# A down-projection whose plain features are split over two rounds of products, with feature reads paced per product and an unscaled residual

## The chip, the cores and the metric

One core of one Trainium2 chip runs the whole kernel. The metric is the device time of one execution in microseconds (us), as the median of several runs. The engines are named as the profile names them: PE is TensorE (matrix products), DVE is VectorE, ACT is ScalarE, POOL is GpSimd and SP is SyncE, which only issues transfers here.

## What is computed

One decoder layer over 1032 tokens (1024 of a prompt, 8 of a sample), 1024 features wide, in float32:

```
h <- LN1(alpha*h + 0.5*SwiGLU_1(h))
h <- LN2(alpha*h + W_o[ sig(g_a)*(A(h) W_ao) + sig(g_r)*(R(h) W_ro) ])
h <- LN3(alpha*h + 0.5*SwiGLU_2(h))

def swiglu(x, w_up, w_down):
    gate, up = jnp.split(x @ w_up, 2, axis=-1)
    return (jax.nn.silu(gate) * up) @ w_down
```

A is sliding-window attention and R is a retention; alpha is 2^(1/4), about 1.189. The hidden width of a SwiGLU is 2816, which is 22 tiles of 128. The change is about the two products with `w_down` (one in each feed-forward part) and about the factor alpha of the residual.

## The kernel before

**Products.** A float32 product is made of three TensorE products of halves: each operand is split into a rounded part `hi` and a rest `lo`, and hi·hi, hi·lo and lo·hi are added. The split of an operand tile is two instructions: ACT copies the tile into `hi` (line 112), then DVE subtracts `hi` from the tile (line 116). A weight half tile (128x512) is loaded by SP into one of 4 buffers `raw`; ACT writes `w_hi` and DVE `w_lo`, into one of 8 slots. A slot is free again when the last product that used its previous weight has run, so the ACT row that writes a `w_hi` waits for PE.

**Quads.** Most of the work runs in a scheme in which seven products stand for eight (Strassen-Winograd). Seven products, numbered 0 to 6, share a quad of four weight halves; three of their seven weight operands are sums of halves, which DVE makes in four instructions (tiles `st`). Their seven token operands lie split in seven buffers TT[0] to TT[6], the tiles T0 to T6. A product is 24 matmuls of 258 columns into one of three PSUM banks `pr`.

**The feed-forward part.** The up-projection ends with hidden tile 21. Its results leave the core's memory: six hidden tiles (groups 0 and 5) go to DRAM as they are (`adr`, plain features), the sixteen tiles of groups 1 to 4 as seven combinations per pair of groups (`tdr`, two rounds of seven features). The down-projection reads them back. It has four parts, in this order of the list `units` (lines 392 to 409):

- 16 plain units `dn` with group 0 (12 matmuls each): 8 for the output tiles d = 4 to 7 (the accumulator `yb`), then 8 for d = 0 to 3 (`ya`);
- round Q0: 4 quads, j = 0 to 3, of seven products `S` (groups 1 and 2);
- round Q1: 4 quads of seven products (groups 3 and 4);
- units `down` with group 5, one per output tile and chunk of tokens.

Each `dn` and `S` unit ends with an evacuation: DVE adds 0.25 times the bank to a half tile of `ya` or `yb`. In a quad the second product's bank is apart; products 0, 2, 4 and 6 follow one another in one bank, each adding to what stands there, and each of them waits until DVE has evacuated the one before.

**The residual.** `ya` and `yb` start as alpha times the residual. `yb` is in place early; `ya` is read back in `start_d` (2064 KB) when the first plain unit is due, and POOL multiplies it by alpha in 12 instructions (`alpha`, line 843).

**Reads and splits of features.** A feature read (`fetch_one`, lines 929 to 942) goes to a buffer that is no longer used. The table `qslot` says which buffer the feature of product i takes; it is the same in both rounds, so a buffer comes free for Q1 when its last product of Q0 has run. `fetch_after` lets a read start after a unit if 3.5 us of the kernel's own time estimate (FETCH) have passed since the last one. Each read starts a generator `split`: an ACT copy and a DVE subtraction for the first half of the tile, then for the second. `features` is called ahead of the product that needs the feature and puts out what is left of its split.

**The order of the work.** The instruction order on each engine is written out by the program itself: a class `E` keeps an estimate of each engine's time, generators are resumed when their time has come (`E.run`), and what an engine's queue holds then is fixed. Engines run their queues strictly in that order.

Of the kernel before, what the change touches and what calls it, by code (L numbers as in the profile page):

```python
# [18 lines left out]
P = 128  # L19
# [16 lines left out]
QUADS = [(1, 2), (3, 4)]  # L36
ORDER = [0, 1] + [GROUPS[g][k] for q in QUADS for k in range(4) for g in q] + GROUPS[5]
# [11 lines left out]
FETCH = 3.5  # L49
# [174 lines left out]
def build(tc, I, O):  # L224
# [3 lines left out]
    with ctx:  # L228
# [136 lines left out]
        def ffn_units(p, r0):  # L365
# [26 lines left out]
            n = 0  # L392
            for i in (1, 0):
                j = add_job(down[0] + i)
                for dd in range(4):
                    for hf in range(2):
                        units.append(dict(kind="dn", p=p, c=0, d=4 * i + dd, dd=dd, hf=hf, jobs=[j], first=n == 0, bank=(0, 2, 1)[n % 3]))
                        n += 1
            for q, (g1, g2) in enumerate(QUADS):
                for j in range(4):  # L400
                    a, b = down[g1] + j, down[g2] + j
                    for i, (x, h) in enumerate(add_quad([(a, 0), (b, 0), (a, 1), (b, 1)])):
                        quad_op[p, "S", q, j, i] = len(ops)
                        ops.append(dict(src=x, quad=h))
                        units.append(dict(kind="S", p=p, c=0, q=q, j=j, i=i, jobs=[]))
# [430 lines left out]
        def end_t(p):  # L836
# [6 lines left out]
            E.spawn(alpha_b())  # L843

        def alpha(t):
            for k in range(4):
                for c in range(3):
                    n0, N = CH[c]
                    E.pscale(t[:, k, n0:n0 + N], t[:, k, n0:n0 + N], ALPHA, n=N)

        def alpha_b():
            yield E.pe + 40.0
            alpha(env["yb"])
# [35 lines left out]
        def start_d(p):  # L889
# [8 lines left out]
            alpha(env["ya"])  # L898

        def end_quads(p):  # L900

            env["st"] = None
            open_banks([pairs.index(pr[i]) for i in (2, 0, 1)])
# [5 lines left out]
        qslot = [[4, 5, 6, 1, 2, 3, 0], [2, 3, 1, 4, 5, 6, 0]]  # L909
        fetches, fstate, rested, splits = [], dict(t=0.0), {}, {}  # L910

        def fill(p):

            res = [(0, ("U", 0), 0, k) for k in range(2)]
            res += [(s, ("U", s), "Q0", qslot[p].index(s)) for s in range(1, 7)]
            res.append((0, "dn", "Q0", 6))
            res += [(qslot[p][i], (0, i), "Q1", i) for i in range(7)]
            return res + [(qslot[p][i], (1, i), 5, 2 * i + k) for i in range(2) for k in range(2)]

        def split(i, hi, lo, n, t):  # L920
# [3 lines left out]
            for k in (0, g):  # L924
                t = E.act(hi[:, k:k + g], f(lo)[:, k:k + g], n=g)
# [3 lines left out]
        def fetch_one():  # L929
            p, i, _, g, k = fetches.pop(0)  # L930
            x = TT[i]
            if g in (0, 5):
                o = k % 2 * 2 * T
                hi, lo = x[:, o:o + T], x[:, o + T:o + 2 * T]
                ds(out=f(lo), in_=adr[p][k + (2 if g else 0)])
# [6 lines left out]
            splits.setdefault((i, g), []).append(E.spawn(split(i, hi, lo, n, E.dma(n * 0.000512))))  # L942

        def fetch_after(u):
# [10 lines left out]
            elif u["kind"] == "S" and u["j"] == 3:  # L955
                rested[u["q"], u["i"]] = True
            elif u["kind"] == "dn" and (u["d"], u["hf"]) == (3, 1):
                rested["dn"] = True
            while fetches and fetches[0][2] in rested and (E.pe > fstate["t"] + FETCH or fetches[0][4] % 2 and fetches[0][3] in (0, 5)):
                fetch_one()  # L960

# [498 lines left out]
        def evac_s(j, i, bank):  # L1460
# [3 lines left out]
            E.stt(yd, bank[:, :, 0:HC], 0.25, yd, ALU.mult, ALU.add, n=HT)  # L1464


        def evac(u, bank):
# [9 lines left out]
            elif kind == "dn":  # L1477
                k = u["hf"] * HT
                yd = v(Y(u["d"], k, k + HT))
                E.stt(yd, bank[:, :, 0:HC], 0.25, yd, ALU.mult, ALU.add, n=HT)  # L1480
            elif kind == "down":
                d = u["d"]
                yd = Y(d, n0, n0 + N)
                t = E.stt(yd, ps, 0.25, yd, ALU.mult, ALU.add, n=N)
# [129 lines left out]
        def before(ui, u):  # L1614
# [69 lines left out]
            if kind == "dn":  # L1684
                if u["first"]:
                    start_d(u["p"])
                features(u["p"], 0, 0)
# [265 lines left out]
```

## Time and profile before

| what | value |
|---|---|
| time, median of 3 runs | 2236.43 us (2235.77 to 2236.72) |
| the profiled execution's own time | 2237.71 us |
| its span, first to last instruction | 2235.9 us |
| PE busy | 2143.2 us, 96% of the span |
| DVE busy | 1483.8 us, 66% |
| ACT busy | 827.0 us, 37% |
| POOL busy | 233.7 us, 10% |
| first down-projection, start of the first plain unit | 467.08 us |
| second down-projection, start of the first plain unit | 1953.96 us |

How to read it: PE is busy nearly all the time, so a change can shorten the kernel only where PE stands still or runs slowly. In the rows of the timeline the first number is the start, the second the length, xN says how many instructions of one shape follow each other, and in brackets stands how long the engine stood idle ahead of them and for whom. "PEclk" is the granted clock of TensorE as a share of the full one.

### The profile page before, as it was taken

How to read it: one execution, taken by the hardware profiler on the slowest of the kernel's cores; microseconds unless marked ns; L12 is line 12 of the kernel's file. 1: busy time of each engine (PE TensorE's matmuls, PEld its weight loads, DVE VectorE, ACT ScalarE, POOL GpSimd, SP SyncE). 2: the span in 40 equal slices, each digit the busy share in tenths (PEclk: the TensorE clock that was granted, in tenths of full speed). 3: DMA queues.
4: the chain of work that ended last, by engine and by line, in shares of the span. 5: the costliest groups of instructions: out<-in, count | busy, mean ns of one | idle time of the engine just before them, and what ended most of it. 6: DMA issues, size and time to landing. Idle time of an engine off the chain costs nothing.

```text
span 2235.9 us, 39516 instructions
## 1 busy us (share of the span) xinstructions
PE 2143.2 (96%) x15865; PEld 2102.5 (94%) x15865; DVE 1483.8 (66%) x2675; ACT 827.0 (37%) x1561; POOL 233.7 (10%) x283
## 2 busy tenths in 40 slices
PE   8999999989899999999999999997999999989896
PEld 8999999989899889999979999997999999989896
DVE  7766666576656886556676747787666666676657
ACT  5333333342322575111324434554333333432323
POOL 1100000010004433111110202011000000010003
PEclk9999999999999999999999999999999999999998
DMA  4322323261421211111253434531332232353322
GB/s 141 107 96 86 113 92 109 73 244 60 171 101 37 66 41 35 44 40 40 77 189 130 139 123 133 185 113 54 103 105 91 96 110 91 133 180 109 118 97 76
DMA packets 111129, 231.81 MB, mean 104 GB/s; under 512 B 13666, under 2 KB 17602, under 8 KB 107090
## 3 DMA queue, kind: packets, MB, share of 16 engines
q1 hardware_dynamic: 110594, 229.24, 30.3%
q8 instruction: 125, 2.05, 0.4%
q14 instruction: 58, 0.48, 0.1%
q0 software_dynamic: 352, 0.05, 0.1%
HBM read 184.44 MB, written 45.84 MB: 103 GB/s over the span
## 4 chain that ended last, share of the span: by engine, by line
PE 55%; DVE 9%; DMA 3%; ACT 2%; issue 2%; POOL 1%; SPq 0%; DVEq 0%; POOLq 0%; ACTq 0%
PE pr L94 28%; PE mb L94 25%; DVE T L116 2%; DVE w_lo L116 1%; PE sb L94 1%; DVE ya L116 1%; DMA raw<-in_w_dram 1%; DVE yb L116 1%; DMA T<-tdr 1%; DVE ln L116 1%; DVE zt L116 1%; PE sb L102 1%; ACT w_hi L112 1%; ACT T L112 0%; DVE st L116 0%
## 5 line engine op out<-in xcount | busy, mean ns | idle before, releaser
L94 PE MATMUL pr<-T,w_hi 128*128 128x258 f32 x7008 | 1151.0, 286 | 54.0 <-DVE T L116 14.1
L94 PEld LDWEIGHTS pr<-T,w_hi 128*128 128x128 f32 x7008 | 979.7, 192 | 65.7 <-DVE T L116 17.2
L94 PE MATMUL pr<-T,w_lo 128*128 128x258 f32 x3504 | 714.8, 286 | 1.3 <-DVE w_lo L116 1.3
L94 PEld LDWEIGHTS pr<-T,w_lo 128*128 128x128 f32 x3504 | 553.0, 192 | 1.8 <-DVE w_lo L116 1.8
L94 PE MATMUL mb<-T,w_hi 128*128 128x384 f32 (+1 forms) x2208 | 528.2, 326 | 1.8 <-DVE yb L116 1.8
L116 DVE TENSOR_TENSOR w_lo<-raw,w_hi 128x512 fp32r<-128x512 f32 x500 | 357.3, 733 | 142.5 <-ACT w_hi L112 141.4
L112 ACT ACTIVATE w_hi<-raw 128x512 fp32r<-128x512 f32 x500 | 304.7, 625 | 270.2 <-PE pr L94 138.4
L94 PEld LDWEIGHTS mb<-T,w_hi 128*128 128x128 f32 x2208 | 380.1, 190 | 8.3 <-issue 4.7
L94 PE MATMUL mb<-T,w_lo 128*128 128x384 f32 (+1 forms) x1104 | 354.7, 321 | 0.0
L94 PEld LDWEIGHTS mb<-T,w_lo 128*128 128x128 f32 x1104 | 208.7, 189 | 0.0
L112 ACT ACTIVATE w_hi<-st 128x512 fp32r<-128x512 f32 x174 | 108.2, 629 | 181.5 <-DVE st L116 88.5
L116 DVE TENSOR_TENSOR a<-pr,a 128x516 f32<-128x516 f32 x87 | 60.5, 696 | 97.6 <-PE pr L94 93.9
L116 DVE TENSOR_TENSOR w_lo<-st,w_hi 128x512 fp32r<-128x512 f32 x174 | 116.0, 688 | 9.0 <-ACT w_hi L112 9.0
L136 POOL TENSOR_SCALAR ya<-ya 128x384 f32<-128x384 f32 (+1 forms) x24 | 16.2, 676 | 834.3 <-DMA ya<-hres 433.4
L112 ACT ACTIVATE a<-pr 128x516 f32<-128x516 f32 x86 | 51.5, 600 | 135.6 <-PE pr L94 135.6
L116 DVE SCALAR_TENSOR_TENSOR ya<-pr,ya 128x516 f32<-128x516 f32 x72 | 49.6, 691 | 76.5 <-PE pr L94 65.8
L112 ACT ACTIVATE T<-T 128x1032 fp32r<-128x1032 f32 (+1 forms) x80 | 72.2, 927 | 64.3 <-DMA T<-tdr 60.4
L116 DVE TENSOR_TENSOR T<-T 128x1032 fp32r<-128x1032 f32 (+1 forms) x80 | 85.1, 1080 | 15.3 <-ACT T L112 15.1
L116 DVE SCALAR_TENSOR_TENSOR yb<-pr,yb 128x516 f32<-128x516 f32 x72 | 49.4, 693 | 54.2 <-PE pr L94 54.2
L112 ACT ACTIVATE th<-a 128x516 f32<-128x516 f32 x43 | 27.3, 636 | 125.6 <-DVE a L116 125.6
L116 DVE SCALAR_TENSOR_TENSOR gt<-gt,mb 128x384 f32<-128x384 f32 (+1 forms) x48 | 24.3, 509 | 59.4 <-PE mb L94 57.8
L116 DVE TENSOR_TENSOR ln<-pr,ln 128x516 f32<-128x516 f32 x43 | 29.9, 695 | 50.7 <-PE pr L94 50.7
(317 smaller groups left out, 2242.9 us busy)
## 6 DMA issues: line engine op xcount, KB each, us to landing
raw<-in_w_dram SPq DMA_DIRECT2D x500, 256.0 KB, 2.9
T<-tdr SPq DMA_DIRECT2D x28, 1032.0 KB, 7.2
tdr<-ya SPq DMA_DIRECT2D x56, 258.0 KB, 3.2
tdr<-s SPq DMA_DIRECT2D x32, 258.0 KB, 2.6
tdr<-m SPq DMA_DIRECT2D x24, 258.0 KB, 3.0
T<-adr SPq DMA_DIRECT2D x12, 516.0 KB, 5.0
out_yp_dram<-zt SPq DMA_DIRECT2D x16, 256.0 KB, 2.0
adr<-m SPq DMA_DIRECT2D x5, 516.0 KB, 4.5
```

What stands on the lines that cost most here:

```text
L94: self.nc.tensor.matmul(out=out, lhsT=lhsT, rhs=rhs, start=start, stop=stop, **kw)
L102: self.nc.tensor.transpose(out=out, in_=in_, identity=ident)
L112: self.nc.scalar.activation(out=out, in_=in_, func=func, scale=scale, **kw)
L116: getattr(self.nc.vector, fn)(**kw)
L136: self.nc.gpsimd.tensor_scalar(out=out, in0=a, scalar1=s, scalar2=1.0, op0=ALU.mult, op1=ALU.mult)
```

## The change

1. The 16 plain units become two halves of 8. The half for `yb` stays ahead of round Q0; the half for `ya` comes between Q0 and Q1. Group 0's two features are read a second time for it (two more reads of 516 KB for each down-projection) into the buffer of Q0's first feature, and split a second time (two reads, two halves each). Round Q0 takes its quads in the order j = 2, 3, 0, 1, so that it begins with `yb`.
2. `qslot` has a row for each round: the buffers are handed round, so that Q1's feature i takes the buffer that Q0's feature i+1 had. The banks of a quad change places.
3. FETCH goes from 3.5 to 2.0, so that a read may follow each product (one takes 2.9 us). A `split` starts 1.5 us later and waits while DVE's estimated time is over 0.5 us ahead of PE's. The features of the next product of a round are put out ahead of the present product's matmuls.
4. The residual stays unscaled: POOL's 24 multiplications of each down-projection go, evacuations multiply by 0.25/alpha, the layer norm's constant is divided by alpha squared, and ahead of LN2 a scalar_tensor_tensor becomes a tensor_tensor.

```diff
+DOWN = 0.25 / ALPHA
-LN_EPS = 1e-5
+LN_EPS = 1e-5 / ALPHA ** 2
+QJ = [(2, 3, 0, 1), (0, 1, 2, 3)]
-FETCH = 3.5
+FETCH = 2.0
...
-            for i in (1, 0):
-                j = add_job(down[0] + i)
+            for q, (g1, g2) in enumerate(QUADS):
+                jj = add_job(down[0] + 1 - q)
                 for dd in range(4):
                     for hf in range(2):
...
-            for q, (g1, g2) in enumerate(QUADS):
-                for j in range(4):
+                for n, j in enumerate(QJ[q]):
...
             ds(out=env["ya"], in_=hres if p else xd[:, 0:4, :])
             E.dma(2.114)
-            alpha(env["ya"])
...
-        qslot = [[4, 5, 6, 1, 2, 3, 0], [2, 3, 1, 4, 5, 6, 0]]
+        qslot = [[[1, 4, 5, 2, 3, 6, 0], [4, 5, 2, 3, 6, 0, 1]], [[1, 2, 3, 4, 5, 6, 0], [2, 3, 4, 5, 6, 0, 1]]]
...
+            s0, s1 = qslot[p]
             res = [(0, ("U", 0), 0, k) for k in range(2)]
-            res += [(s, ("U", s), "Q0", qslot[p].index(s)) for s in range(1, 7)]
-            res.append((0, "dn", "Q0", 6))
-            res += [(qslot[p][i], (0, i), "Q1", i) for i in range(7)]
+            res += [(s, ("U", s), "Q0", s0.index(s)) for s in range(1, 7)]
+            res.append((0, "dn0", "Q0", 6))
+            res += [(s0[0], (0, 0), 1, k) for k in range(2)]
+            res += [(s0[i], (0, i), "Q1", i - 1) for i in range(1, 7)]
+            res.append((s0[0], "dn1", "Q1", 6))
...
             for k in (0, g):
+                while E.eng["dve"] > E.pe + 0.5:
+                    yield E.pe + 0.3
                 t = E.act(hi[:, k:k + g], f(lo)[:, k:k + g], n=g)
...
-            splits.setdefault((i, g), []).append(E.spawn(split(i, hi, lo, n, E.dma(n * 0.000512))))
+            splits.setdefault((i, g), []).append(E.spawn(split(i, hi, lo, n, E.dma(n * 0.000512) + 1.5)))
...
-            E.stt(yd, bank[:, :, 0:HC], 0.25, yd, ALU.mult, ALU.add, n=HT)
+            E.stt(yd, bank[:, :, 0:HC], DOWN, yd, ALU.mult, ALU.add, n=HT)
...
-                E.stt(yd, f(HH(d, n0, N)), ALPHA, ps, ALU.mult, ALU.add, n=N)
-                t = E.stt(yd, f(HL(d, n0, N)), ALPHA, yd, ALU.mult, ALU.add, n=N)
+                E.stt(yd, ps, 1.0 / ALPHA, f(HH(d, n0, N)), ALU.mult, ALU.add, n=N)
+                t = E.tt(yd, yd, f(HL(d, n0, N)), ALU.add, n=N)
...
+            x = units[ui + 1] if ui + 1 < len(units) else u
+            if x["kind"] == "S" and kind == "S" and x["q"] == u["q"]:
+                features(u["p"], qslot[u["p"]][x["q"]][x["i"]], f"Q{x['q']}")
```

What this does to the order on the engines is seen best at the start of the two rounds of the first down-projection. In the rows, `T1_146` to `T3_148` are the feature buffers T1 to T3, `T4_156` to `T6_158` are T4 to T6, and `T0_145` is T0; a row `T<-T` is one half of a feature's split (x2: both halves). `w_hi4_69` is the high part of the weight in slot 4, `w_lo4_77` its rest, `pr0_181` to `pr2_183` are the three banks, `yb_152` and `ya_4889` or `ya_4879` the accumulators.

DVE, around the last plain units ahead of round Q0, before:

```order
L116 TENSOR_TENSOR w_lo7_80<-raw2_83,w_hi7_72 128x512
L116 TENSOR_TENSOR w_lo4_77<-st2_164,w_hi4_69 128x512
L116 SCALAR_TENSOR_TENSOR ya_4889<-pr0_181,ya_4889 128x516
L116 SCALAR_TENSOR_TENSOR ya_4889<-pr2_183,ya_4889 128x516
L116 TENSOR_TENSOR T4_156<-T4_156 128x1032
L116 SCALAR_TENSOR_TENSOR ya_4889<-pr1_182,ya_4889 128x516
L116 TENSOR_TENSOR T4_156<-T4_156 128x1032
```

And after, from behind the evacuation of the eighth plain unit to the evacuation of the second product of Q0:

```order
L118 TENSOR_TENSOR w_lo7_80<-raw1_82,w_hi7_72 128x512
L118 TENSOR_TENSOR w_lo4_77<-raw2_83,w_hi4_69 128x512
L118 TENSOR_TENSOR T1_146<-T1_146 128x1032
L118 TENSOR_TENSOR T4_156<-T4_156 128x1032 x2
L118 TENSOR_TENSOR T2_147<-T2_147 128x1032
L118 TENSOR_TENSOR T3_148<-T3_148 128x1032
L118 SCALAR_TENSOR_TENSOR yb_152<-pr1_182,yb_152 128x516
L118 TENSOR_TENSOR w_lo5_78<-raw3_84,w_hi5_70 128x512
L118 TENSOR_TENSOR T5_157<-T5_157 128x1032
L118 TENSOR_TENSOR T6_158<-T6_158 128x1032
L118 TENSOR_TENSOR T5_157<-T5_157 128x1032
L118 SCALAR_TENSOR_TENSOR yb_152<-pr2_183,yb_152 128x516
```

Before, the splits of Q0's features lay between the evacuations of the second eight plain units. Now they stand behind the evacuation of the eighth, between the products of Q0's first quad. Behind these rows the list goes on with the four sums of the next quad, T6's second half, `w_lo0`, T0's first half, and only then the evacuation of the third product of Q0.

ACT at the same place, before:

```order
L112 ACTIVATE w_hi7_72<-raw2_83 128x512
L112 ACTIVATE w_hi4_69<-st2_164 128x512
L112 ACTIVATE T4_156<-T4_156 128x1032 x2
L112 ACTIVATE T5_157<-T5_157 128x1032 x2
L112 ACTIVATE T6_158<-T6_158 128x1032 x2
L112 ACTIVATE w_hi5_70<-raw3_84 128x512
```

And after:

```order
L114 ACTIVATE w_hi7_72<-raw1_82 128x512
L114 ACTIVATE w_hi4_69<-raw2_83 128x512
L114 ACTIVATE T1_146<-T1_146 128x1032
L114 ACTIVATE T4_156<-T4_156 128x1032
L114 ACTIVATE T2_147<-T2_147 128x1032
L114 ACTIVATE T3_148<-T3_148 128x1032
L114 ACTIVATE T4_156<-T4_156 128x1032
L114 ACTIVATE T5_157<-T5_157 128x1032
L114 ACTIVATE T6_158<-T6_158 128x1032
L114 ACTIVATE w_hi5_70<-raw3_84 128x512
```

Slot 4 holds the weight of the last four plain units, so `w_hi4` can only be written when PE has run the eighth of them; eight halves of features now stand behind it (the list goes on with T5, T6 and T0).

DVE at the start of round Q1, before:

```order
L116 TENSOR_TENSOR w_lo4_77<-st1_163,w_hi4_69 128x512
L116 TENSOR_TENSOR T1_146<-T1_146 128x1032 x2
L116 SCALAR_TENSOR_TENSOR ya_4889<-pr2_183,ya_4889 128x516
L116 TENSOR_TENSOR w_lo5_78<-st0_162,w_hi5_70 128x512
L116 SCALAR_TENSOR_TENSOR ya_4889<-pr0_181,ya_4889 128x516
L116 TENSOR_TENSOR w_lo0_73<-raw2_83,w_hi0_65 128x512
L116 TENSOR_TENSOR T2_147<-T2_147 128x1032 x2
```

And after, from behind the evacuation of the last plain unit:

```order
L118 TENSOR_TENSOR w_lo3_76<-raw3_84,w_hi3_68 128x512
L118 TENSOR_TENSOR w_lo6_79<-raw0_81,w_hi6_71 128x512
L118 TENSOR_TENSOR T4_156<-T4_156 128x1032
L118 TENSOR_TENSOR T5_157<-T5_157 128x1032
L118 SCALAR_TENSOR_TENSOR ya_4879<-pr1_182,ya_4879 128x516
L118 TENSOR_TENSOR T2_147<-T2_147 128x1032
L118 TENSOR_TENSOR w_lo7_80<-raw1_82,w_hi7_72 128x512
L118 TENSOR_TENSOR T3_148<-T3_148 128x1032
L118 TENSOR_TENSOR T6_158<-T6_158 128x1032
L118 TENSOR_TENSOR T0_145<-T0_145 128x1032
L118 TENSOR_TENSOR T2_147<-T2_147 128x1032
L118 SCALAR_TENSOR_TENSOR ya_4879<-pr2_183,ya_4879 128x516
```

Before, each feature of Q1 was split as a whole ahead of its own product. Now the first halves of four features and more second halves come in a row, ahead of the first quad's second evacuation; the four sums, T3's second half, `w_lo4`, and the second halves of T6 and T0 follow ahead of its third.

On SP the reads of Q0's first six features move ahead of the first plain unit's residual read; the read of the seventh (into T0) stays behind a plain feature's write and the residual's read. Outside the two down-projections nothing changes place.

More of the change, by code (lines that the diff above doesn't have):

```diff
@@ L391, in ffn_units @@
             units.extend(first[:2] + rest[:2] + first[2:] + rest[2:])
-            n = 0
-            for i in (1, 0):
-                j = add_job(down[0] + i)
+            for q, (g1, g2) in enumerate(QUADS):
+                jj = add_job(down[0] + 1 - q)
                 for dd in range(4):
                     for hf in range(2):
-                        units.append(dict(kind="dn", p=p, c=0, d=4 * i + dd, dd=dd, hf=hf, jobs=[j], first=n == 0, bank=(0, 2, 1)[n % 3]))
-                        n += 1
-            for q, (g1, g2) in enumerate(QUADS):
-                for j in range(4):
+                        n = 2 * dd + hf
+                        units.append(dict(kind="dn", p=p, c=0, d=4 * (1 - q) + dd, dd=dd, hf=hf, jobs=[jj], part=q, n=n,
+                                          bank=((0, 2, 1), (1, 0, 2))[q][n % 3]))
+                for n, j in enumerate(QJ[q]):
                     a, b = down[g1] + j, down[g2] + j
@@ L404, in ffn_units @@
                         ops.append(dict(src=x, quad=h))
[L405 removed]
+                        units.append(dict(kind="S", p=p, c=0, q=q, j=j, i=i, n=n, jobs=[]))
             dj = [(add_job(down[5] + i), [(2 * i + dd, dd) for dd in range(2)]) for i in range(4)]
@@ L842, in end_t @@
                 open_ut()
[L843 to L853, printed above, removed]
         def early_t():
@@ L931, in fetch_one @@
             x = TT[i]
-            if g in (0, 5):
+            if g in (0, 1, 5):
                 o = k % 2 * 2 * T
                 hi, lo = x[:, o:o + T], x[:, o + T:o + 2 * T]
-                ds(out=f(lo), in_=adr[p][k + (2 if g else 0)])
+                ds(out=f(lo), in_=adr[p][k + (2 if g == 5 else 0)])
                 n = T
@@ L954, in fetch_after, with dn_slot @@
                 rested["U", u["i"]] = True
-            elif u["kind"] == "S" and u["j"] == 3:
+            elif u["kind"] == "S" and u["n"] == 3:
                 rested[u["q"], u["i"]] = True
-            elif u["kind"] == "dn" and (u["d"], u["hf"]) == (3, 1):
-                rested["dn"] = True
-            while fetches and fetches[0][2] in rested and (E.pe > fstate["t"] + FETCH or fetches[0][4] % 2 and fetches[0][3] in (0, 5)):
+            elif u["kind"] == "dn" and u["n"] == 7:
+                rested[f"dn{u['part']}"] = True
+            while fetches and fetches[0][2] in rested and (E.pe > fstate["t"] + FETCH or fetches[0][4] % 2 and fetches[0][3] in (0, 1, 5)):
                 fetch_one()
+        def dn_slot(u):
+            return qslot[u["p"]][0][0] if u["part"] else 0
         def features(p, i, g):
@@ L1684, in before @@
             if kind == "dn":
-                if u["first"]:
+                if u["part"] + u["n"] == 0:
                     start_d(u["p"])
-                features(u["p"], 0, 0)
+                features(u["p"], dn_slot(u), u["part"])
             if kind == "S":
-                features(u["p"], qslot[u["p"]][u["i"]], f"Q{u['q']}")
+                features(u["p"], qslot[u["p"]][u["q"]][u["i"]], f"Q{u['q']}")
+            x = units[ui + 1] if ui + 1 < len(units) else u
+            if x["kind"] == "S" and kind == "S" and x["q"] == u["q"]:
+                features(u["p"], qslot[u["p"]][x["q"]][x["i"]], f"Q{x['q']}")
             if kind == "down":
@@ L1693, in before @@
                 for i in range(2):
-                    features(u["p"], qslot[u["p"]][i], 5)
+                    features(u["p"], qslot[u["p"]][1][i], 5)
             if kind == "k":
@@ L1732, in product @@
             if u["kind"] in ("P", "S"):
-                xs = [TT[u["i"] if u["kind"] == "P" else qslot[u["p"]][u["i"]]]]
+                xs = [TT[u["i"] if u["kind"] == "P" else qslot[u["p"]][u["q"]][u["i"]]]]
                 fresh = u["i"] in (0, 1, 3)
```

16 lines of the change are left out of this document (8 added, 8 removed).

## The prediction

> **What bounds the kernel now.** First the page's shares and its chain of waits:
>
> ```profile
> PE 2143.2 (96%) x15865; PEld 2102.5 (94%) x15865; DVE 1483.8 (66%) x2675; ACT 827.0 (37%) x1561; POOL 233.7 (10%) x283
> PE 55%; DVE 9%; DMA 3%; ACT 2%; issue 2%; POOL 1%; SPq 0%; DVEq 0%; POOLq 0%; ACTq 0%
> ```
>
> PE is the bound, so only its idle or slow time can be won. The change touches the two down-projections, so I read those by stage. The rows run from the first plain unit to the first product of round Q0's second quad, through the other 24 products up to Q1, and through Q1's first quad; three rows for each projection:
>
> ```profile
> 467.08:512.49 45.41, 37.41 (x289) 35.11 (x288) 38.57 (x52) 18.43 (x23) 8.13 (x12) 1.00 0.58 207
> 512.49:581.95 69.46, 69.46 (x574) 69.46 (x575) 41.49 (x64) 17.93 (x27) 0.00 (x0) 1.00 0.29 98
> 581.95:619.67 37.72, 28.12 (x172) 26.70 (x171) 25.25 (x31) 13.97 (x18) 0.00 (x0) 0.82 0.41 147
> 1953.96:1998.61 44.65, 38.10 (x288) 36.57 (x288) 38.33 (x52) 18.54 (x23) 8.09 (x12) 0.96 0.58 210
> 1998.61:2068.07 69.46, 69.46 (x577) 69.46 (x578) 41.57 (x64) 18.02 (x27) 0.00 (x0) 1.00 0.29 98
> 2068.07:2103.40 35.33, 26.56 (x171) 24.89 (x169) 24.86 (x31) 13.98 (x18) 0.00 (x0) 0.86 0.43 158
> ```
>
> The columns are length, then busy time and instructions of PE, weight loads, DVE, ACT and POOL, then the clock, the DMA share and GB/s. In the middle row PE never rests: 24 products in 69.46 us are 2.894 us each, so a plain unit (half the matmuls) is 1.447. From the first plain unit to the end of Q1's first quad there are 16 plain units and 35 products: 16 × 1.447 + 35 × 2.894 = 124.4 us. The three rows take 152.6 and 149.4 us. So 28.1 and 25.0 us are lost, **53.1 us** together. That is the stock the change can draw on. What PE waits for there, first projection, then second:
>
> ```profile
> PE pr L94 <- DVE T L116: 5.8, 4, 2.3
> PE pr L94 <- DVE ya L116: 5.6, 6, 2.9
> PE pr L94 <- ACT T L112: 3.0, 2, 1.5
> ...
> PE pr L94 <- DVE ya L116: 6.2, 5, 3.3
> PE pr L94 <- DVE T L116: 5.8, 4, 2.3
> ```
>
> Two causes are seen: evacuations into `ya`, and splits of features. The first is the residual, in the timelines of POOL, DVE, SP and ACT:
>
> ```profile
> 488.74 8.94 POOL L136 TENSOR_SCALAR ya<-ya 128x384 f32<-128x384 f32 x12 [399.31 <-DMA ya<-in_x_dram]
> ...
> 489.86 0.70 DVE L116 SCALAR_TENSOR_TENSOR ya<-pr,ya 128x516 f32<-128x516 f32 x1 [4.74 <-POOL ya L136]
> ...
> 481.18 0.33 SPq L896 DMA_DIRECT2D ya<-in_x_dram  x1
> 481.61 1.61 SPq L939 DMA_DIRECT2D T<-tdr  x3
> ...
> 491.05 2.02 ACT L112 ACTIVATE T<-T 128x1032 fp32r<-128x1032 f32 x2 [8.15 <-DMA T<-tdr]
> ```
>
> The second is Q1's first quad, where a feature is split only when its product is due (PE, then ACT and DVE):
>
> ```profile
> 590.53 0.64 PE L94 MATMUL pr<-T,w_hi 128*128 128x258 f32 x4
> ...
> 591.25 0.65 PE L94 MATMUL pr<-T,w_hi 128*128 128x258 f32 x4
> ...
> 594.39 0.58 PE L94 MATMUL pr<-T,w_hi 128*128 128x258 f32 x2 [2.01 <-DVE T L116]
> ...
> 595.20 1.06 PE L94 MATMUL pr<-T,w_hi 128*128 128x258 f32 x4
> ...
> 596.49 1.06 PE L94 MATMUL pr<-T,w_hi 128*128 128x258 f32 x4
> ...
> 598.65 0.40 PE L94 MATMUL pr<-T,w_hi 128*128 128x258 f32 x2
> 601.34 0.67 PE L94 MATMUL pr<-T,w_hi 128*128 128x258 f32 x2 [2.30 <-DVE T L116]
> ...
> 605.60 0.63 ACT L112 ACTIVATE w_hi<-st 128x512 fp32r<-128x512 f32 x1 [5.37 <-issue]
> 606.14 2.00 ACT L112 ACTIVATE T<-T 128x1032 fp32r<-128x1032 f32 x2
> ...
> 607.22 2.38 DVE L116 TENSOR_TENSOR T<-T 128x1032 fp32r<-128x1032 f32 x2
> ```
>
> The chain per product is: PE ends, ACT writes a `w_hi` whose slot PE has just left, then both halves of T, then DVE. After a wait of 2.01 us PE runs at half pace: six matmuls take 596.49 − 595.20 = 1.29 us instead of 591.25 − 590.53 = 0.72. From 594.39 to 599.05 it does 24 matmuls that are worth 2.89, so such a cold stretch costs about 1.7 us beside its wait.
>
> **The change part by part.** Steps, from rows above and these:
>
> ```profile
> 472.32 1.29 DVE L116 TENSOR_TENSOR w_lo<-st,w_hi 128x512 fp32r<-128x512 f32 x2
> ...
> 477.01 1.89 DVE L116 SCALAR_TENSOR_TENSOR yb<-pr,yb 128x516 f32<-128x516 f32 x3
> ...
> L116 DVE TENSOR_TENSOR st<-st,raw 128x512 f32<-128x512 f32 x58 | 40.3, 695 | 2.0
> ```
>
> Two T halves in a row take 2.38 us, that is 1.15 each; ACT's take 2.00, that is 0.96. Three evacuations take 1.89, two `w_lo` 1.29, and a sum of halves is as long as these: 0.60 for each as its step in the queue.
>
> *The unscaled residual.* POOL's rows go, and the first evacuation into `ya` comes one round later than its read. The 4.74 us that DVE waited, and PE's wait behind it, are gone: `ya` is next needed after 14 products (14 × 2.9 = 40 us later). That the multiplications of `yb` go costs and brings nothing; they ran beside other work, far ahead of use. The changed rows ahead of LN2 stand beside PE's work:
>
> ```profile
> L116 DVE SCALAR_TENSOR_TENSOR ya<-T,ya 128x384 f32<-128x384 f32 x8 | 4.5, 559 | 0.3
> L116 DVE TENSOR_TENSOR ln<-ln 128x384 f32<-128x384 f32 x12 | 9.1, 757 | 0.7 <-POOL ln L132 0.7
> ```
>
> There are 24 of them. At worst each goes from 559 to 757 ns, 4.8 us of DVE; I take nothing, since DVE is idle a third of the span.
>
> *Round Q0.* This part decides. Zero is the end of the eighth plain unit. The order puts on DVE, ahead of the evacuation of Q0's third product: the evacuation of the eighth unit, `w_lo7` and `w_lo4`, ten T halves, four sums, `w_lo5` and `w_lo0`, and three evacuations. That is 0.6 + 1.2 + 11.5 + 2.4 + 1.2 + 1.8 = 18.7 us. It starts 0.2 us after zero (PE's end to DVE), and waits once for ACT: ACT cannot write `w_hi4` before zero, so it reaches T4's second half after 0.6 + 5 × 0.96 = 5.4 us, when DVE has been free since 0.2 + 0.6 + 1.2 + 2 × 1.15 = 4.3. Sum: 0.2 + 18.7 + 1.1 = 20.0 us. The fifth product waits for that evacuation; PE has only four products to fill the time, 4 × 2.894 = 11.6. So PE loses 8.4 us in this quad, of which some already at the third product, which waits for T5's second half (DVE ends it at 13.6, the third product would be through by 8.7). Behind the fifth product DVE has few halves left, and nothing else is late.
>
> *Round Q1.* The same count holds with zero at the end of the second half of the plain units: ten T halves, four sums, four `w_lo`, the last unit's and three products' evacuations, 18.7 us again. DVE waits about 0.9 for `w_hi7`, which stands on ACT behind `w_hi6` and six halves (0.6 + 6 × 0.96 + 0.6 = 7.0, DVE free at 6.1). So the fifth product starts at 0.2 + 18.7 + 0.9 = 19.8, and 8.2 are lost.
>
> *Cold clock.* PE's pace matters only where PE is what is late. In the first four products DVE is, with 8 us to spare; behind the fifth product's wait a cold stretch counts. I take 1 us for each round, as the wait there is about 2.4 us (between 0 and 1.7).
>
> *The halves of plain units.* The first half is as now, with these waits of PE in the first projection:
>
> ```profile
> 471.85 0.75 PE L94 MATMUL pr<-T,w_hi 128*128 128x258 f32 x4 [1.89 <-DVE m L116]
> ...
> 474.26 0.75 PE L94 MATMUL pr<-T,w_hi 128*128 128x258 f32 x4 [0.69 <-DVE yb L116]
> ...
> 482.83 0.76 PE L94 MATMUL pr<-T,w_hi 128*128 128x258 f32 x4 [0.47 <-DVE yb L116]
> PE pr L94 <- DVE yb L116: 0.7, 1, 0.7
> ```
>
> That is 3.0, and in the second projection 0.7 (last row); I take 3 and 1. The second half's features are read again and split during Q0's later quads, where DVE is busy 41.49 of 69.46 us: four halves of a plain feature, each half as long as a T half (0.6), cost nothing. If one came late, PE would wait its 0.6. The two reads (1 MB) meet a DMA share of 0.29.
>
> *Reads paced closer.* Q0's six reads now stand on SP ahead of the residual's read, and first halves are split beside the plain units; they pass only weight loads, of which PE has eight slots in stock. Q1's reads can follow each product, and all but the last features land during Q0's last quad. This removes the chain per feature; what is late next is DVE, as counted.
>
> Sum: first projection 3 + 8.4 + 8.2 + 2 = 21.6, second 1 + 8.4 + 8.2 + 2 = 19.6, together 41.2 against 53.1: a gain of 11.9. From the profiled execution: 2237.7 − 11.9 = 2225.8. The median lies 1.3 below that execution, so **2224.5 us**.
>
> The Trainium skill (TensorE: Matmul & The Clock Gate, "Why this matters for your kernels") says that PE drops to half speed after an idle gap of over about 3 us, a whole window of idleness. By that rule no cold stretch would follow waits of 2.4 us, and the sum would be 4 us lower, 2220.5. The trace here shows half pace behind 2.01 and 2.30 us, so I keep the 4 us.
>
> Bounds for this case: without cold stretches and without DVE's waits for ACT a round costs 7.3 (18.9 − 11.6), and with 0.7 for each projection's plain units 30.6 are lost, a gain of 22.5: 2214. With one more cold stretch of 1.7 in each round and 3 us at the plain units of both it is 41.2 + 6.8 + 2 = 50, a gain of 3: 2233. The case's own range is 2214 to 2233.
>
> **The rivals.** 0.2% (4.5 us) is about what a measurement of this kernel can tell from no change.
>
> *No change, around 2236.* Each round has three waits; I took 1 us of cold clock. If the stretches of 1.7 behind two of the three count in full, that is 2.4 more in each round, 9.6 in all, and leaves a gain of 2.3 (2234); if all three do, 4.1 more, 16.4 in all, it is slower by 4.5 (2241). I put the case at 2236. For it: the rows above run cold behind every 2 us wait. Against it: DVE is late there, and a slow PE fits into its delay. 14 in 100.
>
> *Slower, 2243.* The read of Q0's seventh feature stands on SP behind the residual's read. In the trace the first read behind the residual's is issued at 481.61 and its feature reaches ACT at 491.05, 9.4 us later. The residual's read is issued at 481.18, 14.1 us after the first plain unit starts; zero is 8 × 1.447 + 0.7 = 12.3 us after it. So T0 reaches ACT about 14.1 + 0.4 + 9.4 − 12.3 = 11.6 after zero. T0's first half stands in DVE's queue at 18.3, ahead of everything behind it. From 6.7 us later on (a plain feature's write that lands late holds the residual's read back) every us stops DVE and so PE. A landing 16 us later than worked out in each projection costs 2 × 9.3 = 18.6 against the gain of 11.9: slower by 6.7. For it: SP stood 8.75 us between that write's issue and the residual's read:
>
> ```profile
> 472.43 0.33 SPq L1437 DMA_DIRECT2D adr<-m  x1
> ```
>
> Against it: those 8.75 us are in the 14.1 already. 8 in 100.
>
> *Bigger gain, about 2200.* If the splits hide as the order of reads would allow, only a first wait of some 3 us is left in each round: 4 × 3 + 2 × 2 = 16 are lost and 37 gained. Against it: 18.7 us of DVE work stand in the queue in a fixed order. 8 in 100.
>
> **How the numbers follow.** The forecast has 70 in 100, no change 14, slower 8, bigger gain 8. Faster by over 0.2%: nearly all of the forecast's part (its last us reaches past 2232) and the bigger gain, 77; within 0.2%: 14; slower: 9. The range goes from 2212, 2 us under the forecast's lower bound for what a run differs from the median (1.3) and its rounding, to 2237, over the middle of the no-change case; it leaves out the bigger gain, the slower case and the no-change case's upper end, together below 20.
>
> **What would show it.** In the changed profile: the timeline of PE waits three times in each round's first quad, some 4, 2 and 2 us, for T and an evacuation; DVE is busy without a break for about 19 us from the last plain unit of each half; the windows from the first plain unit to Q1's second quad, summed, are some 12 us shorter; no wait for POOL's `ya`. Wrong would be: DVE idle in these bursts (then ACT or a read is late), waits for DMA at T0, or a PE that does not stand at the fifth product.

## The result, and the profile after

The changed kernel takes 2224.45 us (median of 4 runs, 2219.80 to 2227.07) against 2236.57 before: a ratio of 0.9943 with a 95% interval of 0.9926 to 0.9960, so faster by 12.1 us. The forecast was 2224.5. The profiled execution is the fastest of the four, 2219.80 us with a span of 2218.0. First its shares:

```profile
PE 2132.1 (96%) x15865; PEld 2092.5 (94%) x15865; DVE 1486.7 (67%) x2683; ACT 831.6 (37%) x1569; POOL 200.9 (9%) x235
```

PE has the same instructions and is busy 11 us less: fewer of them run at half pace. Then the stages, with the plain units where they now are. For each projection the rows are: first half of the plain units and Q0's first quad; the rest of Q0 and the second half of the plain units; Q1's first quad. The last row is the first half of the plain units alone.

```profile
468.39:509.94 41.55, 35.13 (x265) 33.61 (x264) 34.81 (x45) 16.07 (x21) 0.00 (x0) 0.96 0.45 172
509.94:582.78 72.84, 72.80 (x604) 72.61 (x602) 44.91 (x69) 18.48 (x29) 0.00 (x0) 1.00 0.43 153
582.78:611.48 28.70, 22.71 (x170) 21.87 (x169) 25.80 (x31) 15.67 (x19) 0.00 (x0) 0.94 0.21 75
1944.57:1984.58 40.01, 34.62 (x265) 33.58 (x265) 34.88 (x45) 16.03 (x21) 0.00 (x0) 0.96 0.48 184
1984.58:2057.33 72.75, 72.70 (x603) 72.52 (x601) 44.91 (x69) 18.57 (x29) 0.00 (x0) 1.00 0.43 153
2057.33:2086.02 28.69, 22.73 (x170) 21.90 (x169) 25.80 (x31) 15.66 (x19) 0.00 (x0) 0.94 0.22 77
...
468.39:481.04 12.65, 11.86 (x98) 11.65 (x97) 10.24 (x15) 1.40 (x4) 0.00 (x0) 1.00 0.83 309
```

Without waits and half pace these would be 31.8, 72.4 and 20.3 us. So the first projection loses 9.7 + 0.4 + 8.4, the second 8.2 + 0.4 + 8.4: 35.5 us, where it was 53.1. POOL's column is empty. What PE waits for, first projection, then second:

```profile
PE pr L96 <- DVE T L118: 6.6, 5, 2.9
PE pr L96 <- DVE yb L118: 3.8, 3, 1.5
PE pr L96 <- DVE ya L118: 1.9, 1, 1.9
...
PE pr L96 <- DVE T L118: 7.1, 4, 2.9
PE pr L96 <- DVE ya L118: 1.9, 1, 1.9
PE pr L96 <- ACT T L114: 1.5, 1, 1.5
PE pr L96 <- DVE yb L118: 0.8, 1, 0.8
```

And the place on which the forecast rested, Q0's first quad: PE's waits, then DVE's queue, then ACT's and SP's.

```profile
473.69 0.75 PE L96 MATMUL pr<-T,w_hi 128*128 128x258 f32 x4 [0.79 <-DVE yb L118]
484.34 0.51 PE L96 MATMUL pr<-T,w_hi 128*128 128x258 f32 x2 [1.19 <-DVE T L118]
...
490.71 0.48 PE L96 MATMUL pr<-T,w_hi 128*128 128x258 f32 x2 [1.52 <-DVE yb L118]
492.36 0.51 PE L96 MATMUL pr<-T,w_hi 128*128 128x258 f32 x2 [1.17 <-DVE T L118]
...
492.95 1.03 PE L96 MATMUL pr<-T,w_hi 128*128 128x258 f32 x4
...
501.28 0.74 PE L96 MATMUL pr<-T,w_hi 128*128 128x258 f32 x4 [1.50 <-DVE yb L118]
...
481.24 0.70 DVE L118 SCALAR_TENSOR_TENSOR yb<-pr,yb 128x516 f32<-128x516 f32 x1 [0.75 <-PE pr L96]
481.85 1.28 DVE L118 TENSOR_TENSOR w_lo<-raw,w_hi 128x512 fp32r<-128x512 f32 x2
483.05 2.37 DVE L118 TENSOR_TENSOR T<-T 128x1032 fp32r<-128x1032 f32 x2
486.44 3.52 DVE L118 TENSOR_TENSOR T<-T 128x1032 fp32r<-128x1032 f32 x3 [1.01 <-ACT T L114]
...
500.54 0.69 DVE L118 SCALAR_TENSOR_TENSOR yb<-pr,yb 128x516 f32<-128x516 f32 x1
...
481.00 0.64 ACT L114 ACTIVATE w_hi<-raw 128x512 fp32r<-128x512 f32 x1 [5.17 <-PE pr L96]
481.54 6.78 ACT L114 ACTIVATE T<-T 128x1032 fp32r<-128x1032 f32 x7
...
477.23 0.33 SPq L886 DMA_DIRECT2D ya<-in_x_dram  x1
481.24 0.32 SPq L933 DMA_DIRECT2D T<-tdr  x1
```

The eighth plain unit ends at 481.0; ACT writes the `w_hi` that had to wait for it and then seven halves of features in one go (T x7, 6.78 us); DVE's queue runs from 481.24 to 501.2 with one break of 1.01 us, for ACT; and the fifth product starts at 501.28, 20.2 us behind the last plain unit. T0's read, issued at 481.24, is in time.

### The profile page after: what moved, and what is told of

Read it like the earlier page. It is cut to its first block, busy times and chain, and to the rows that moved or that the text cites. A ratio compares the mean times of both kernels' runs of the same rounds, so it can differ in the third digit from the quotient of the medians.

```text
span 2218.0 us, 39430 instructions
## 1 busy us (share of the span) xinstructions
PE 2132.1 (96%) x15865; PEld 2092.5 (94%) x15865; DVE 1486.7 (67%) x2683; ACT 831.6 (37%) x1569; POOL 200.9 (9%) x235
## 4 chain that ended last, share of the span: by engine, by line
PE 79%; DVE 11%; ACT 3%; DMA 3%; issue 2%; POOL 1%; SPq 0%; DVEq 0%; POOLq 0%; ACTq 0%
PE pr L96 52%; PE mb L96 25%; DVE T L118 3%; DVE w_lo L118 2%; DMA raw<-in_w_dram 2%; PE sb L96 1%; DVE ya L118 1%; DVE yb L118 1%; ACT T L114 1%; DVE ln L118 1%; DVE zt L118 1%; DVE st L118 1%; DMA yb<-in_x_dram 1%; PE sb L104 1%; ACT w_hi L114 1%
## 5 line engine op out<-in xcount | busy, mean ns | idle before, releaser
L134 POOL TENSOR_TENSOR ln<-ya 128x384 f32<-128x384 f32 (+1 forms) x6 | 6.8, 1130 | 793.3 <-DVE ya L118 793.2
```

The source lines that it names most:

```text
L134: self.nc.gpsimd.tensor_tensor(out=out, in0=a, in1=b, op=op)
```

## The experiments

Three theories. **Queue theory**: in the first quad of each round PE loses what DVE has in its queue ahead of the third evacuation, beyond four products of PE; what the order puts there decides. **Residual theory**: the gain is the wait for POOL's multiplications. **Split theory**: the gain is the plain units as cover in each round. Times are medians; the kernel before, timed beside them, took 2236.36 (first four), 2235.86 (next four) and 2237.03 us (last three). The last column is PE's loss in the two down-projections of the profiled execution, read as in the forecast (from the first plain unit to the end of Q1's first quad, less 124.4 us for each; the end found by counting 1032 matmuls, good to about half a us). It was 53 in the kernel before and 35.5 in the changed kernel's first trace. A median and this column do not always agree, since executions differ by some us outside the down-projections and in where PE runs at half pace.

| kernel | us | ratio to before, 95% interval | PE's loss, us |
|---|---|---|---|
| changed, once more | 2225.31 | 0.9953 (0.9935 to 0.9970) | 36 |
| before, unscaled residual | 2229.56 | 0.9975 (0.9963 to 0.9988) | 47 |
| changed, plain units together | 2228.23 | 0.9966 (0.9955 to 0.9978) | 44 |
| changed, no holds in split | 2200.69 | 0.9843 (0.9823 to 0.9864) | 14 |
| changed, two subtractions cut | 2216.97 | 0.9906 (0.9888 to 0.9925) | 33 |
| changed, FETCH 3.5 | 2224.74 | 0.9946 (0.9930 to 0.9962) | 40 |
| changed, scaled residual | 2227.21 | 0.9964 (0.9950 to 0.9979) | 43 |
| before, FETCH 2.0 | 2210.48 | 0.9883 (0.9864 to 0.9901) | 26 |
| changed, no hold for DVE's backlog | 2204.38 | 0.9860 (0.9839 to 0.9881) | 16 |
| before, FETCH 2.0, unscaled residual | 2206.80 | 0.9877 (0.9857 to 0.9896) | 23 |
| changed, no holds, plain units together | 2209.63 | 0.9884 (0.9865 to 0.9903) | 22 |

**The changed kernel once more.** No edit.

> The changed kernel once more, to see how far its executions lie apart. The queue theory (PE loses in each round what DVE has in its queue ahead of the evacuation of the third product, beyond four products of PE) expects the same waits at the same places in every execution, so a median of 2222 to 2226 and differences between executions only where PE runs at half pace behind such a wait. If instead the reads decide (a late read of a feature), the waits change place from execution to execution and waits for a DMA are seen.

2225.31 us, with the same waits. PE's wait rows at three places, which answer to 473.69 and 501.28 above and to 1949.84 in the first trace:

```profile
475.46 0.75 PE L96 MATMUL pr<-T,w_hi 128*128 128x258 f32 x4 [0.79 <-DVE yb L118]
486.11 0.51 PE L96 MATMUL pr<-T,w_hi 128*128 128x258 f32 x2 [1.19 <-DVE T L118]
...
503.05 0.75 PE L96 MATMUL pr<-T,w_hi 128*128 128x258 f32 x4 [1.62 <-DVE yb L118]
...
1954.40 0.74 PE L96 MATMUL pr<-T,w_hi 128*128 128x258 f32 x4 [0.78 <-DVE yb L118]
```

From the first to the third row it is 27.59 us in both executions (501.28 − 473.69 as well). Of the 5 us between the executions 1.8 lie ahead of the first down-projection and 2.8 between the two of them. The first down-projection is the same to the hundredth up to Q1's fifth product; the second takes 0.7 us longer, because PE runs at half pace for longer in its Q0.

**The unscaled residual alone.** The kernel before with

```
-            alpha(env["ya"])
-            E.spawn(alpha_b())
-            E.stt(yd, bank[:, :, 0:HC], 0.25, yd, ALU.mult, ALU.add, n=HT)
+            E.stt(yd, bank[:, :, 0:HC], DOWN, yd, ALU.mult, ALU.add, n=HT)
```

and the rest of the change's fourth part.

> The kernel before with the fourth part of the change alone: the residual unscaled, the 24 multiplications on POOL gone, all else as before. Queue theory: the plain units still stand behind the residual's read, which lands when it landed before; only POOL's first multiplication, about 1 us, goes from each down-projection, so 1 to 4 us faster, 2233 to 2236. Rival, the residual theory (most of the gain is the wait for POOL's multiplications): 8 to 12 us faster, 2225 to 2229.

2229.56, so 6.8 us: between the two, and more than I gave it. DVE in this kernel, then in the kernel before at the same place:

```profile
488.26 0.70 DVE L117 SCALAR_TENSOR_TENSOR ya<-pr,ya 128x516 f32<-128x516 f32 x1 [3.34 <-DMA ya<-in_x_dram]
488.87 0.68 DVE L117 TENSOR_TENSOR w_lo<-raw,w_hi 128x512 fp32r<-128x512 f32 x1
...
491.75 1.23 DVE L117 TENSOR_TENSOR T<-T 128x1032 fp32r<-128x1032 f32 x1 [0.39 <-ACT T L113]
```

```profile
490.47 0.97 DVE L116 TENSOR_TENSOR w_lo<-raw,w_hi 128x512 fp32r<-128x512 f32 x1
...
493.49 1.39 DVE L116 TENSOR_TENSOR T<-T 128x1032 fp32r<-128x1032 f32 x1
494.79 0.68 DVE L116 SCALAR_TENSOR_TENSOR ya<-pr,ya 128x516 f32<-128x516 f32 x1
```

DVE's wait for `ya` is 1.4 us shorter, about as counted, and stays for the read; PE's wait behind it goes from 2.87 to 1.47 us, and in the second projection only from 3.33 to 2.89. What I had not counted: while POOL multiplied, DVE's rows with two inputs from SBUF took 0.97 and 1.39 us instead of 0.68 and 1.23; the evacuation (0.68), with one input from PSUM, did not. The Trainium skill (SBUF — State Buffer, "Who interferes with whom") says just that: a DVE instruction with two SBUF inputs contends with a GpSimd instruction that reads SBUF, one with at most one (outside the modes that use both of its port pairs) does not. The trace agrees, with the numbers above. How much of the 6.8 us it makes is not shown. By stage about 5 us are gained at the plain units, where POOL worked; of these, PE's waits for `ya` are 1.8, and in the second projection the half pace behind that wait is gone too. Another 1.2 us are gained in the first projection's Q1, where POOL did nothing: a wait of 2.01 us there is not followed by half pace as it was before.

**All plain units ahead of Q0.** The changed kernel with one loop over the two halves ahead of the loop over the rounds, and without the second read.

```
-            for q, (g1, g2) in enumerate(QUADS):
+            for q in range(2):
                 jj = add_job(down[0] + 1 - q)
...
+            for q, (g1, g2) in enumerate(QUADS):
                 for n, j in enumerate(QJ[q]):
...
-            res += [(s0[0], (0, 0), 1, k) for k in range(2)]
-            res.append((s0[0], "dn1", "Q1", 6))
+            res.append((s0[0], (0, 0), "Q1", 6))
```

> The changed kernel with all sixteen plain units ahead of round Q0 again, so without the second read of group 0; pacing, look-ahead, buffers handed round and unscaled residual stay. Queue theory: the order puts eleven halves of features on DVE ahead of Q0's third evacuation (ten with the split) and seven ahead of Q1's (ten with the split), and the units for ya wait some 2 to 3 us for the residual's read: about 9 + 3 us lost at Q0 and 4 at Q1 for each projection, 32 in all against 36 in the changed kernel: within 5 us of it, 2217 to 2229. Rival, the split theory (the gain comes from giving each round plain units as cover): 8 to 12 us slower than the changed kernel, 2232 to 2236.

2228.23: 3 us slower than the changed kernel, inside the queue theory's range at its upper edge and away from the split theory's. But the time alone flatters the queue theory. The count of 32 us was too low: the two down-projections lose about 44 in this execution, 8 more than in the changed kernel, which is nearly what the split theory expected. Of the 8 us, 2 are PE's waits (25.7 us against 23.6); most of the others are half pace, which here follows the waits for an evacuation in Q0 and Q1 as well (the clock is 0.983 against 0.986 in the two profiled executions). So this run does not settle whether the plain units matter as cover; the last experiment says more.

**No holds in split.** The changed kernel with

```
-                while E.eng["dve"] > E.pe + 0.5:
-                    yield E.pe + 0.3
...
-E.dma(n * 0.000512) + 1.5)
+E.dma(n * 0.000512))
```

> The changed kernel without the two holds in split: a feature is split as soon as the estimate says that its read has landed, whatever DVE's backlog is. In the order only three halves of features are left ahead of Q0's third evacuation and three ahead of Q1's, where there were eight to ten. Queue theory: the wait at the fifth product goes; what is left in Q0 is the seventh feature, which lands about 11.6 us behind the last plain unit and whose two halves stand ahead of the third evacuation, 3 to 4 us, and about 1 us in Q1: 10 to 14 us lost in all against 36, so 2197 to 2206. Rival (the holds are needed: earlier splits come in the way of evacuations of the products that run then): the waits move ahead of the rounds, into the last quads, and the time is 2220 to 2230.

2200.69, 24.6 us under the changed kernel and 36 under the kernel before. DVE around the first half of the plain units, then PE's only waits from the last of these units to the end of Q0's first quad:

```profile
476.79 1.23 DVE L118 TENSOR_TENSOR T<-T 128x1032 fp32r<-128x1032 f32 x1
477.93 0.69 DVE L118 SCALAR_TENSOR_TENSOR yb<-pr,yb 128x516 f32<-128x516 f32 x1
478.54 2.37 DVE L118 TENSOR_TENSOR T<-T 128x1032 fp32r<-128x1032 f32 x2
480.82 0.69 DVE L118 SCALAR_TENSOR_TENSOR yb<-pr,yb 128x516 f32<-128x516 f32 x1
...
490.81 2.38 DVE L118 TENSOR_TENSOR T<-T 128x1032 fp32r<-128x1032 f32 x2
...
481.57 0.75 PE L96 MATMUL pr<-T,w_hi 128*128 128x258 f32 x4 [1.17 <-DVE yb L118]
486.90 0.72 PE L96 MATMUL pr<-T,w_hi 128*128 128x258 f32 x4 [0.38 <-DVE yb L118]
```

The splits now fill the gaps that DVE had between the evacuations of the plain units, and only T0's two halves (490.81) come late. The price is paid at the plain units: a wait of 1.17 us in the first half, of 0.87 in the second and of 0.73 right behind it, and in all about 6 us lost there in each projection instead of 1.5. Q1's first quad then loses nothing. So the hold, which is part of the change, had made the burst that the forecast counted.

**Two subtractions cut.** The changed kernel with the order kept and DVE's work made less; part of the low halves of two features is left out.

```
+                m = 8 if cut and k else g
-                E.tt(lo[:, k:k + g], f(lo)[:, k:k + g], f(hi)[:, k:k + g], ALU.subtract, n=g)
+                E.tt(lo[:, k:k + m], f(lo)[:, k:k + m], f(hi)[:, k:k + m], ALU.subtract, n=g)
```

> The changed kernel in which the subtraction for the second half of the third and of the fourth feature of each round writes 8 columns instead of 1032, so that part of the low halves of these features is left out; the order of all instructions is that of the changed kernel. It takes 2 x 1.1 us off DVE's queue ahead of the third evacuation of each round. Queue theory: the fifth product starts about 2 us earlier in three of the four rounds and the third or fourth in the other, 6 to 9 us in all against the changed kernel (2225): 2216 to 2219. Rival (PE waits for ACT, a read or the clock there, DVE only being busy at the same time): less than 2 us, 2223 or more.

2216.97, 8.3 us under the changed kernel. PE in Q0, to be held against 486.11 and 503.05 above:

```profile
484.43 0.51 PE L96 MATMUL pr<-T,w_hi 128*128 128x258 f32 x2 [1.19 <-DVE T L118]
...
499.25 0.76 PE L96 MATMUL pr<-T,w_hi 128*128 128x258 f32 x4 [2.04 <-DVE yb L118]
```

14.82 us from row to row instead of 16.94: the fifth product comes 2.12 us earlier for 2.1 us less on DVE. This shows that DVE's queue, not ACT, a read or the clock, sets that point. In both Q1 the fifth product comes 2.1 us earlier too. The time is another matter: in these three rounds PE now runs at half pace behind its fifth product, which takes 1.2 to 1.5 us back each time, and the down-projections gain only about 3 us in this execution. The rest of the 8.3 us lies outside them, so that the range was met is in part chance.

**FETCH back at 3.5 in the changed kernel.**

> The changed kernel with FETCH back at 3.5, so that reads follow every second product. The order then has 9, 10, 8 and 10 halves of features ahead of the third evacuation of the four rounds, where the changed kernel has 10, 10, 9 and 10. Queue theory: the waits stay where they are, within 3 us of the changed kernel, 2222 to 2228. Rival, the read theory (the gain comes from features that land earlier): waits for reads or ACT's copies come back at the later products of each round, 6 to 10 us slower, 2231 to 2235.

2224.74, no difference to the changed kernel in time. By stage the down-projections lose about 4 us more, most of it in the first projection's Q0, where PE waits 2.50 us for ACT's copy of a feature: what the read theory expected, but too little for the time to show. (In the changed kernel's trace the third of the four rounds has seven halves ahead of the third evacuation, not nine.)

**The scaled residual put back in the changed kernel.**

> The changed kernel with the scaled residual put back: POOL's 24 multiplications for each down-projection and the old rows ahead of LN2; everything else is as changed. Queue theory: ya is needed only after round Q0's first two quads, so the multiplications are hidden: within 2 us of the changed kernel, 2223 to 2227. Rival (the multiplications cost DVE or PE time wherever they run, since taking them out of the kernel before brought 6.8 us): 5 to 8 us slower, 2230 to 2233.

2227.21, about 2 us slower than the changed kernel (2225.31), with intervals that overlap; just above the queue theory's range and short of the rival's. The multiplications do not hide: they fall on Q0's burst. POOL, then DVE:

```profile
486.20 12.70 POOL L138 TENSOR_SCALAR ya<-ya 128x384 f32<-128x384 f32 x12 [395.28 <-DMA ya<-in_x_dram]
...
490.51 0.68 DVE L118 SCALAR_TENSOR_TENSOR yb<-pr,yb 128x516 f32<-128x516 f32 x1
491.11 0.95 DVE L118 TENSOR_TENSOR w_lo<-raw,w_hi 128x512 fp32r<-128x512 f32 x1
491.99 4.32 DVE L118 TENSOR_TENSOR T<-T 128x1032 fp32r<-128x1032 f32 x3
```

Three T halves take 4.32 us here and 3.52 without POOL, and POOL's twelve rows 12.70 instead of the 8.94 that they took beside the plain units before. In the first Q0 the fifth product comes 2.2 us later behind the first wait for T. By stage the down-projections lose about 7 us more than in the changed kernel: some 4 in the two Q0, and 3 in the two Q1, where POOL is done and PE runs at half pace behind its fifth product. The median shows 2 of these 7; which is nearer to the lasting cost stays open.

**One constant in the kernel before.**

```
-FETCH = 3.5
+FETCH = 2.0
```

> The kernel before with one constant changed, FETCH from 3.5 to 2.0. The order then puts five halves of features ahead of Q1's third evacuation, where the changed kernel has ten, and Q1's features land about 11 us before they are due. Queue theory: the waits for the residual at the plain units stay, 10.7 and 9.9 us, and Q1 loses 1 to 3 us instead of 17.4 and 15.1: 23 to 27 us lost instead of 53, so 2206 to 2213, better than the whole change. Rival (the change needs its parts together: buffers handed round, look-ahead, holds): the chain of one feature after the other stays in Q1 and the time is 2228 or more.

2210.48: 25.4 us faster than the kernel before, and 15 us faster than the whole change. PE's waits in the first projection's Q1, which were seven:

```profile
PE pr L94 <- DVE ya L116: 3.0, 1, 3.0
```

The total came as counted, its two parts did not. Q1 loses about 5 us in each projection, twice what I gave it (half pace follows the one wait); the plain units and Q0's first products lose about 7.5 and 8 instead of 10.7 and 9.9, where I had expected no change.

**Without the hold for DVE's backlog only.**

```
-                while E.eng["dve"] > E.pe + 0.5:
-                    yield E.pe + 0.3
```

> The changed kernel without the hold in split that waits for DVE's estimated backlog; the later start by 1.5 us stays. The order then has three or four halves of features ahead of the third evacuation of each round, as without both holds. Queue theory: as without both, 2198 to 2205. Rival (the later start by 1.5 us is what gathers the splits behind the plain units): 2215 or more.

2204.38: this hold is the one that gathers the splits; the later start by 1.5 us costs about 4 more by the medians, about 2 in the down-projections.

**FETCH 2.0 and the unscaled residual in the kernel before.** Both edits above.

> The kernel before with two edits: FETCH from 3.5 to 2.0, and the unscaled residual. The one alone brought 25.4 us, the other 6.8. Queue theory: they act at different places (Q1's first quad, and the plain units), so they add up: 2201 to 2207. Rival (with the reads earlier the plain units wait for the residual's read itself, so that the multiplications no longer matter): at most 3 us better than the first alone, 2207 to 2211.

2206.80, 3.7 us better than FETCH alone: in the first theory's range and at the edge of the rival's. The two do not add up in full; with reads at 2.0 PE's waits for `ya` at the plain units were already down (0.5 and 0.7 us in the first projection). How much is overlap and how much scatter stays open.

**No holds, and all plain units ahead of Q0.** The edits of the third and the fourth kernel together.

> The changed kernel without both holds in split and with all sixteen plain units ahead of round Q0 again. The units for ya wait for the residual's read once more, 2 to 3 us in each projection, and five halves of features stand ahead of Q1's third evacuation instead of three, 1 to 2 us. Queue theory: 6 to 9 us slower than without the holds (2200.7), 2206 to 2210. Rival (splitting the plain units brings nothing once the splits are spread): 2203 or less.

2209.63, 8.9 us slower than without the holds alone, and about 8 by stage. Splitting the plain units is worth that much once nothing else is in the way, and 3 us by the median as the change has it (8 by stage, as above). But not for the reason that I gave first: the sixteen units together lose 5.6 us in each projection, no more than the two halves do, and PE does not wait for the residual. The difference is Q1's first quad, which loses 4 and 5 us here and nothing with the second half of the units ahead of it. To that extent the split theory holds.

## Why the prediction was right, point by point

- *Q0's burst, 8.4 us in each projection.* First projection: the third evacuation was to end 20.0 us behind the last plain unit; the fifth product started at 20.2, and 8.6 were lost (9.7 less 1.1 for the plain units). The mechanism is shown by the cut subtractions and by the kernels without the hold. Second projection: 7.1 (8.2 less 1.1), with waits of another kind:

```profile
1970.73 0.51 PE L96 MATMUL pr<-T,w_hi 128*128 128x258 f32 x2 [1.53 <-ACT T L114]
1973.13 0.51 PE L96 MATMUL pr<-T,w_hi 128*128 128x258 f32 x2 [1.89 <-DVE T L118]
...
1974.49 1.06 PE L96 MATMUL pr<-T,w_hi 128*128 128x258 f32 x4
```

  I had costed the second projection by the first one's order. The buffers are handed round in another order there, seven halves instead of ten stand ahead of the third evacuation, and nothing waits at the fifth product. So this 7.1 is near the 8.4 by chance: it is 4.6 us of waits at the first and fourth product, about 1 us of smaller gaps, and half pace (below).
- *Q1's burst, 8.2 each.* 8.4 and 8.4 measured; the count of 18.7 us for DVE held.
- *Plain units, 3 and 1.* 1.1 in both (0.79 us is one wait). The wait of 1.89 us for the up-projection's last tile did not come back; sized too high by 2.
- *Cold clock, 1 us a round.* 0 in three rounds: behind the fifth product's waits of 1.50, 1.93 and 1.91 us PE ran at full pace at once. Half pace did come ahead of the fifth product (492.95: 1.03 for four matmuls that take 0.64), but that fits into DVE's delay, as argued. In the second projection's Q0 it falls on the fifth product itself (1974.49 above), which takes 4.3 us instead of 2.9, and no wait behind it takes that up: up to 1.4 us, part of the 7.1. So the 4 us were too high by 2.6 or more. That they were so low is chance as much as anything: in kernels next to this one half pace does follow the fifth product, for 1.2 to 1.6 us, behind a wait of the same length. The fifth product of the first Q1, changed kernel, then with the scaled residual:

```profile
602.80 0.75 PE L96 MATMUL pr<-T,w_hi 128*128 128x258 f32 x4 [1.93 <-DVE ya L118]
```

```profile
605.17 1.20 PE L96 MATMUL pr<-T,w_hi 128*128 128x258 f32 x4 [1.90 <-DVE ya L118]
```

  The Trainium skill's limit of about 3 us for an idle gap (TensorE: Matmul & The Clock Gate, "Why this matters for your kernels") would have given this term as 0, which is right for three rounds of the four; it does not give the half pace behind 1.52 and 1.17 us here, nor that behind 2.01 us before.
- *The sum.* 41.2 forecast, 35.5 measured in the profiled execution and about 36 in the second trace: the terms above make some 17 us of gain instead of 11.9. That the median came out at the forecast all the same is luck, from outside the down-projections. The rest of the program took 1933.9 us in the trace of the kernel before; in the two traces of the changed kernel it took 1933.5 (the execution of 2219.80) and about 1938 (that of 2225.19, near the median). In the four kernels built on the kernel before it is 1931 to 1934, in the nine runs of the changed kernel and its variants 1933.5 to 1939. By these the change may cost about 3 us there (an estimate from the two averages), for which the forecast has no term; the kernel before scatters by more (2227 to 2244 us in 23 runs), and no run shows it apart.
- *The rows of the 53.1.* The first row of each projection ends at Q0's fifth product (288 matmuls are 16 units of 12 and 4 products of 24), not at the second quad's first, as the text has it. The middle row then holds the 24 products by which it was divided, so the 53.1 stands.
- *The residual.* The wait for POOL went, as said. What the forecast left out is that the multiplications slow DVE's rows while they run; taking them out alone brought 6.8 us, of which that is a part that no run separates. Whether `yb`'s multiplications cost nothing was not tried by itself.
- *Reads paced closer.* Said to remove Q1's chain per feature. It does; the kernel before with FETCH 2.0 alone shows it for 25.4 us. But in the changed kernel the pace itself no longer matters (FETCH 3.5: same time). That the hold for DVE's backlog takes the gain back is likely, since it goes with the hold, but no run has the changed kernel with FETCH 3.5 and without the hold.
- *The rivals.* The late read of T0 did not happen (issued at 481.24, and no engine waited for it). The "bigger gain, about 2200" is what the change gives without its own holds, 2200.69.
- *The signs.* DVE was busy for about 19 us in three of the bursts and PE stood at their fifth product, as said. The waits were not "some 4, 2 and 2 us" in each: Q0 has five of 0.25 to 1.5 us in the first projection, Q1 three of 1.1, 2.9 and 1.9. The windows are 17 us shorter, not 12.

## What to carry to other kernels

Count, from the order of an engine's queue, the work that stands ahead of the one instruction that releases the bound engine; that count gave the loss to within 0.3 us in three bursts of four. When the time meets the forecast, see whether the stage moved by as much: here the stages gave 17 us and the median 12. A rule that holds side work back while an engine is estimated to be late does not take the work away: it gathers it at the next place where someone must wait, here at a price of 20 to 25 us. And try each constant of a change by itself on the kernel before: one of them was worth twice the whole.

## What the runs showed of the hardware

While POOL's TENSOR_SCALAR rows on SBUF ran, DVE's rows with two SBUF inputs took longer: `w_lo` 0.97 us instead of 0.68, a T half 1.39 instead of 1.23, three of them 4.32 instead of 3.52; evacuations out of PSUM stayed at 0.68. POOL's twelve rows took 8.94 us beside the plain units and 12.70 in the burst, where DVE has more such rows.

PE's half pace does not go by the length of one wait alone. In the kernel before it came behind 2.01 us (594.39) and stayed away behind 2.87 (490.61) and 2.03 (2079.86); in the changed kernel it came behind two waits of 1.52 and 1.17 us that ended 1.65 us apart and stayed away behind 1.93, where a variant has it behind 1.90. What decides it the runs do not show.
